# Rotary half swap by a copy and four transfers, and token factors spread by transpositions, in a two-block transformer kernel

## The chip, the cores and the metric

The kernel runs on one core of one Trainium2 chip. The metric is the device time of one execution in microseconds; lower is better. Several runs are taken, and their median is quoted.

## The reference, cut to what matters

512 tokens of width 1024 go through two transformer blocks in float32. Two pieces of it matter here: the rotary turn of queries and keys in the first block, and the root-mean-square norms, which stand in both.

```python
def rmsnorm(x, g):
    return x * rsqrt(mean(x * x, axis=-1) + EPS) * g

def apply_rope(t, cos, sin):            # t: 64 features of one half head
    t1, t2 = jnp.split(t, 2, axis=-1)   # 32 and 32
    return jnp.concatenate([t1 * cos - t2 * sin, t1 * sin + t2 * cos], axis=-1)

def first_block(x, ...):
    h = rmsnorm(x, norm_mix_g); proj = h @ w_in
    p, q, k, v = split(proj, [512, 1024, 1536])
    pool_out = multiscale_pool(p, pool_w, pool_scale)
    q, k = apply_rope(q), apply_rope(k)             # 4 heads, 2 x 64 features each
    attn_out = diff_attention(q, k, v, lam, ...)
    x = x + concat([pool_out, attn_out]) @ w_o
    u = causal_dwconv(rmsnorm(x, norm_ffn_g) @ w_up, conv_w, conv_b)
    x = x + (silu(gate) * val) @ w_down
    return rmsnorm(x, norm_final_g)
# second block: feed forward, sparse attention and recurrence side by side,
# feed forward, gated embedding; each with a norm before and a norm behind it
```

## The kernel before, in words

Features lie on the 128 partitions and the 512 tokens along the row, so a block of 128 output features is one PSUM bank of 128x512. The phases in the names of tiles are mixa (mixer of the first block), ffna (its feed forward), fin (its last norm), ffn (the two feed forwards of the second block), mixb (its mixer) and ple (the end). Each float32 weight is split into two float32r parts, hi by a cast on ScalarE (ACT) and lo by a subtraction on VectorE (DVE), in `chunk()` (line 550); each activation likewise in `split()` (line 565). A block of features is then three matmuls for each 128 rows of the weight (`three()`, line 577).

A norm's factor is a value for each token. It is made with tokens on partitions: a matmul with a column of ones sums the squares (`colsum()`, line 672), DVE scales it, GpSimd (POOL) raises it to the power -0.5 (`pow()`, line 679), and `bcast()` (line 696) spreads it back along the row, the same on every partition. For each column of 128 tokens `bcast()` issues one float32 matmul: the column, broadcast to 128x128, is the stationary operand, and the identity moves. It is called with four columns in first_mix, first_ffn, final_norm, second_mix and in each of the two ffn, and with two columns for each half of the tokens in each of the three `renorm()` (line 719): 6 x 4 + 3 x 2 x 2 = 36 products.

`rope()` (line 773) makes the rotary turn of one block of 128 features: two half heads of 64, each of two groups of 32. It needs the block with those groups swapped in pairs. The PSUM block p is split into hi (ACT) and lo (DVE), two matmuls with a permutation matrix `permr` as stationary operand add up the swapped block in another PSUM bank, and DVE makes three passes: p by cos, swapped by sin, and their sum. It runs eight times in first_mix, for query and key of four heads; `permr` is loaded by the SP queue and cast by ACT in `later()` (line 510).

`attention()` (line 800) takes the turned query and key of a head: score products, the maximum on DVE, exponents on ACT, transpositions on TensorE (PE), and the products with the values. Beside the heads, first_mix has the value product (`tokens()`, line 621), four pooling groups and the output product.

No order of work is written by hand. The calls of `Net` are recorded in a `Plan` (line 161). `simulate()` (line 250) is a list scheduler over a cost for each instruction (lines 207 to 233) and a lag between engines (lines 148 and 149): on every engine it takes next the instruction that can start first, and among those that can start at once the one with the smallest key. A DMA costs its issuing queue 470 ns, lands after its bytes at 380 B/ns and 1700 ns more. It runs twice, first with weights for nothing and then with weights placed by what the first pass found, and `write()` emits each engine's instructions in that order. At run time every engine works strictly through its own list. All of them are emitted from line 444, so the profile's rows are told apart by their tiles, and all tiles of 128x512 in SBUF are named slot.

Of the kernel before, what the change touches and what calls it, by code (L numbers as in the profile page):

```python
# [13 lines left out]
OP = mybir.AluOpType  # L14
# [23 lines left out]
class View:  # L38
    """a tile, or a part of one, that gets its place when the program is written out"""
# [22 lines left out]
    def parts(self):  # L62
        b = self.base
        if b.parts is None:
            return [b]
        return [p for p, some in zip(b.parts, (self.dummy.min() < b.at, self.dummy.max() >= b.at)) if some]
# [58 lines left out]
class Base:  # L125
# [5 lines left out]
    def halve(self, at):  # L131
        """from here on the columns before and behind this one are written and read apart"""
        self.at, self.parts = at, [Part(), Part()]
# [27 lines left out]
class Plan:  # L161
    """records instructions, orders them by a model of the core's engines, then writes them out"""
# [8 lines left out]
    def add(self, engine, call, args, kw):  # L171
# [38 lines left out]
        if o.call[1] == "dma_start":  # L210
            o.bytes = int(np.prod(out.dummy.shape if isinstance(out, View) else ins[0].dummy.shape)) * 4
            o.cost, o.lag = 470, 1700
        else:
            o.bytes = 0
            o.lag = 200
            psum = any(v.base.pool == "ps" for _, v in views)
            if engine == "tensor":
                r = all(v.base.dt == F32R for v in ins)
                wide = args[1].n
                o.cost = 3 + (128 * 2 if call == "transpose" else max(n, 2 * wide) if r else 4 * max(n, wide)) / 2.4  # L220
            elif engine == "scalar":
                o.cost = (51 if psum else 93) + n / 1.2 + 93 * sum(k in ("bias", "scale", "accum_out") for k, _ in views)
                f = [x for x in list(args) + list(kw.values()) if isinstance(x, AF)]
                o.func = SETS.get(f[0]) if f else None
            elif engine == "vector":
                fast = not psum and call in ("tensor_copy", "tensor_scalar", "memset")
                cols = sum(v.n == 1 < n for v in ins) if call in ("scalar_tensor_tensor", "tensor_scalar") else 0
                o.cost = 69 + 61 * cols + max([n] + [v.n for v in ins]) / (1.92 if fast else 0.96)
                if call == "tensor_tensor_reduce":
                    o.cost += 270  # L230
            else:
                per = {"memset": 1, "affine_select": 1, "tensor_tensor": 2.6, "tensor_copy": 4}.get(call, 2)
                o.cost = 230 + n * per / 1.2 + (n * 165 if kw.get("op") == OP.pow else 0)
# [3 lines left out]
    # ordering  # L237
# [12 lines left out]
    def simulate(self, first):  # L250
        """list scheduling: sets o.start; the order of starts"""
# [195 lines left out]
class Net:  # L447
# [8 lines left out]
    # tiles  # L456
# [6 lines left out]
    def halved(self, x, at=T // 2):  # L463
        x.base.halve(at)
        x.dummy = np.broadcast_to(np.arange(x.dummy.shape[1], dtype=np.int16), x.dummy.shape)
        return x
# [18 lines left out]
    # constants  # L485
    def setup(self):
# [16 lines left out]
        for _ in range(WARM):  # opens the clock gate of the array  # L503
            nc.tensor.matmul(p, self.ident, self.ident, start=True, stop=True)
# [5 lines left out]
    def later(self):  # L510
        """what the first products do not wait for"""
# [3 lines left out]
        perm = self.t("perm", 1, (P, P))  # L515
        nc.sync.dma_start(perm, a["perm"])
        self.perm = self.c([P, P], "permr", F32R)
        nc.scalar.copy(self.perm, perm)
# [7 lines left out]
    def held(self, w, K, behind):  # L526
        """like chunk(), in slots: the parts of K blocks"""
# [21 lines left out]
    # weights: two float32r parts whose sum is the float32 weight  # L549
# [15 lines left out]
    def split(self, x, g=None, to=None):  # L565
        """x (times the column g) in two float32r parts"""
# [16 lines left out]
    def dots(self, p, q, k, s, t, L):  # L583
        """queries t..L on partitions, keys before L"""
        (qh, ql), (kh, kl) = q, k
        for i, (x, y) in enumerate(((qh, kh), (qh, kl), (ql, kh))):
            self.nc.tensor.matmul(p, x[s, t:L], y[s, :L], start=i == 0, stop=i == 2)

    def block(self, xs, w, p=None):
        """one block of 128 output features in PSUM; w: [P, K * 128] in DRAM"""  # L590
# [12 lines left out]
    def both(self, xs, ws, ps, held=None):  # L603
        """blocks of 128 output features: step by step all of them for one half of the tokens"""
# [16 lines left out]
    def tokens(self, xs, w, n, whole=False, cut=False):  # L621
        """n output features, tokens on partitions: four PSUM banks; w: [chunks, P, k * n]; whole: so many blocks of
        tokens at a time; cut: the last block by halves of the features"""
# [34 lines left out]
    # norms; with a side: for one half of the tokens  # L658
    def sumsq(self, acc, x, scale=1.0, side=None):
        """acc: the sums of squares, made by the first call for each side"""  # L660
# [23 lines left out]
    def mean(self, p, scale=1.0 / 1024, under=None, out=None):  # L684
        """p * scale + EPS (times under)"""
# [10 lines left out]
    def bcast(self, r, keep=False):  # L696
        """column values on tokens -> [P, n * 128], the same on every partition"""
        nc = self.nc
        p = self.sm()[:, :r.n * P]
        for c in range(r.n):  # L700
            nc.tensor.matmul(p[:, c * P:(c + 1) * P], r[:, c:c + 1].to_broadcast([P, P]), self.ident,
                             start=True, stop=True)
# [6 lines left out]
    def prenorm(self, g):  # L709
        """split parts of h * g; the mean square with EPS, and its root's inverse for each token"""  # L710
# [8 lines left out]
    def renorm(self, ys, acc, g, under, gpre, late):  # L719
        """h += g * norm(ys), where ys lack the factor under ** -0.5; then prenorm(gpre); both by halves, each when  # L720
        late() has made its part of ys"""
# [17 lines left out]
    # first block  # L739
# [33 lines left out]
    def rope(self, p, cos, sin):  # L773
        nc = self.nc
        q, u = self.slot(), self.slot()
        hi, lo = self.split(p)
        pp = self.sm()
        nc.tensor.matmul(pp, self.perm, hi, start=True, stop=False)
        nc.tensor.matmul(pp, self.perm, lo, start=False, stop=True)
        nc.vector.tensor_tensor(u, p, cos, op=OP.mult)  # L780
        nc.vector.tensor_tensor(q, pp, sin, op=OP.mult)
# [3 lines left out]
    def diff_lambda(self):  # L785
# [12 lines left out]
        return lam  # minus lambda  # L798
# [35 lines left out]
    def headnorm(self, po):  # L834
        """the inverse root of the mean square of each token, for four blocks of tokens"""
# [7 lines left out]
    def turned(self, o):  # L843
        """tokens on partitions -> features on partitions"""
# [93 lines left out]
    def final_norm(self, gnext):  # L938
        """h <- norm(h) * g, with the next norm's split parts and factor"""
# [20 lines left out]
    # second block  # L960
# [92 lines left out]
    def select_keys(self, b, qi, kT, widx):  # L1053
        """0 on the selected keys of query block b, -NEG elsewhere"""
# [79 lines left out]
    def gated(self, p, rs):  # L1134
        """silu(p * rs)"""
# [6 lines left out]
    def recurrence(self, h, q, f, v, gate, masks):  # L1142
        """per chunk of 128 tokens: products of f over ever longer runs of tokens; a pair of tokens s < t meets
        at the level where they lie in the two halves of one run"""
# [177 lines left out]
    def ple(self, xs, r):  # L1322
        """tokens on partitions"""
# [81 lines left out]
def constants():  # L1405
# [9 lines left out]
    perm = (p[:, None] == (p[None, :] ^ 32)).astype(f)  # L1415
# [8 lines left out]
    return {"cf": cf, "perm": perm, "onehot": onehot, "masks": np.concatenate(ms, 1).astype(np.uint32)}  # L1424


def pack(i):
    i = {k: np.asarray(v) for k, v in i.items()}

    def blocks(w):  # L1430
        """[K*128, M*128] -> [M, 128, K*128]"""
# [3 lines left out]
    def halves(w):  # L1435
        """blocks of the upper and of the lower half of the rows"""
# [3 lines left out]
    def wide(w, nch):  # L1440
        """[1024, n] -> [chunks, 128, k*n]"""
# [75 lines left out]
```

## Time and profile before

| | |
|---|---|
| median of 3 runs | 1773.06 us (1772.69 to 1775.02) |
| span of the profiled execution | 1772.8 us, 22576 instructions |
| PE busy | 1759.4 us (99%), 8882 matmul records |
| DVE, ACT, POOL busy | 1033.4 us, 715.1 us, 49.3 us |
| mean granted TensorE clock | 0.998 |
| DMA | 162.47 MB, all of the kernel's own on the queue of SP |

For the profiled execution the profile gives the span, from its first to its last instruction, and no other time; the median of the runs is 0.26 us above that span. A matmul's record is longer than the time until the next matmul can start, since matmuls are pipelined: what an instruction costs PE is read from the distance between the starts of neighbours, not from its record. In names of matmuls the moving operand stands first behind the arrow and the stationary one second.

### The profile page before, as it was taken

To read this page: it belongs to the slowest core of one execution; us is meant where nothing else is said; L and a number is where in the kernel's file an instruction comes from. 1 tells how busy PE (TensorE), PEld (TensorE's weight loads), DVE (VectorE), ACT (ScalarE), POOL (GpSimd) and SP (SyncE) were. 2 spreads that over 40 slices of the span, in tenths; PEclk is the share of its full clock that TensorE was granted. 3 is DMA by queue.
4 is the path that set the end of the run, shared out by engine and by line. 5 is a ranking of instruction groups with operands and counts; after the bars stand their busy time and mean duration, and the time that the engine had idled before them with its cause. 6 is when DMAs were issued, how large, how long until landed. Compare 5 with 4: busy or idle time off the path is not lost.

```text
span 1772.8 us, 22576 instructions
## 1 busy us (share of the span) xinstructions
PE 1759.4 (99%) x8882; PEld 1476.8 (83%) x8882; DVE 1033.4 (58%) x1820; ACT 715.1 (40%) x1248; POOL 49.3 (3%) x68
## 2 busy tenths in 40 slices
PE   9999999999999999999999999999999999999998
PEld 7778888888888888888898888788899888888896
DVE  7886776367655432343488999553657432343475
ACT  5664444234443322322355334553345322322364
POOL 0021000000000000000010000000000000000000
PEclk9999999999999999999999999999999999999999
DMA  5212232332233223332342321013331323322331
GB/s 201 72 53 92 94 96 77 113 107 96 77 103 106 95 73 106 107 97 83 111 130 71 95 84 49 13 48 95 97 130 49 104 75 101 112 95 80 113 105 60
DMA packets 51690, 162.47 MB, mean 92 GB/s; under 512 B 5936, under 2 KB 7552, under 8 KB 51584
## 3 DMA queue, kind: packets, MB, share of 16 engines
q1 hardware_dynamic: 51584, 161.04, 28.9%
q8 instruction: 69, 1.13, 0.3%
q14 instruction: 37, 0.30, 0.1%
HBM read 158.89 MB, written 2.12 MB: 91 GB/s over the span
## 4 chain that ended last, share of the span: by engine, by line
PE 94%; DVE 4%; ACT 0%; issue 0%; DMA 0%; SPq 0%; POOL 0%; POOLq 0%; DVEq 0%; ACTq 0%
PE ffn.mm L444 41%; PE ffna.mm L444 20%; PE mixb.mm L444 15%; PE mixa.mm L444 7%; PE mixb.sm L444 5%; PE ple.mm L444 3%; DVE mixb.slot L444 2%; PE mixa.sm L444 2%; DVE mixb.m L444 0%; PE ffn.sm L444 0%; DMA mixa.wr_52:2_113<-in_w1qk 0%; SPq L444 0%; PE ple.sm L444 0%; PE fin.sm L444 0%; DVE mixa.dsum L444 0%
## 5 line engine op out<-in xcount | busy, mean ns | idle before, releaser
L444 DVE TENSOR_TENSOR ffn.slot<-ffn.slot,ffn.mm 128x512 f32<-128x512 f32 (+1 forms) x68 | 42.4, 625 | 177.2 <-PE ffn.mm L444 176.5
L444 DVE TENSOR_TENSOR ffn.slot<-ffn.mm,ffn.slot 128x512 f32<-128x512 f32 x44 | 30.3, 691 | 110.4 <-PE ffn.mm L444 109.6
L444 PE MATMUL mixb.sm<-mixb.slot,mixb.slot 128*128 128x64 f32 (+6 forms) x496 | 73.6, 308 | 1.0 <-ACT mixb.slot L444 0.5
L444 DVE TENSOR_TENSOR mixb.slot<-mixb.slot,mixb.slot 128x256 f32<-128x256 f32 (+3 forms) x143 | 67.3, 495 | 11.6 <-ACT mixb.slot L444 11.0
L444 PEld LDWEIGHTS mixb.sm<-mixb.slot,mixb.slot 128*128 128x128 f32 (+1 forms) x496 | 61.1, 190 | 12.2 <-issue 3.3
L444 DVE SCALAR_TENSOR_TENSOR ffna.slot<-ffna.slot,cols,ffna.slot 128x511 f32<-128x511 f32 x88 | 65.8, 748 | 3.1 <-ACT ffna.slot L444 1.3
L444 DVE TENSOR_TENSOR ffna.slot<-ffna.mm,ffna.slot 128x512 f32<-128x512 f32 x44 | 30.3, 689 | 46.4 <-PE ffna.mm L444 45.8
L444 ACT ACTIVATE ffn.slot<-ffn.slot 128x512 f32<-128x512 f32 (+1 forms) x68 | 39.2, 578 | 40.0 <-DVE ffn.slot L444 39.8
L444 DVE TENSOR_TENSOR ffn.slot<-ffn.slot,ffn.slot 128x512 fp32r<-128x512 f32 (+2 forms) x94 | 52.0, 562 | 5.0 <-ACT ffn.slot L444 4.6
L444 ACT COPY mixb.slot<-mixb.sm 128x128 f32<-128x128 f32 (+6 forms) x75 | 27.1, 376 | 43.3 <-PE mixb.sm L444 43.0
L444 DVE TENSOR_TENSOR ffna.slot<-ffna.slot,ffna.slot 128x512 f32<-128x512 f32 (+1 forms) x51 | 35.3, 691 | 14.7 <-ACT ffna.slot L444 13.8
L444 DVE TENSOR_TENSOR mixb.slot<-mixb.mm,mixb.slot 128x512 f32<-128x512 f32 (+1 forms) x28 | 19.3, 690 | 41.7 <-PE mixb.mm L444 40.5
L444 ACT ACTIVATE ffna.slot<-ffna.slot,cols 128x512 f32<-128x512 f32 x44 | 35.8, 815 | 2.6 <-DVE ffna.slot L444 1.9
L444 ACT CAST ffna.slot<-ffna.slot 128x512 fp32r<-128x512 f32 x22 | 13.7, 621 | 52.3 <-DVE ffna.slot L444 52.3
L444 DVE TENSOR_TENSOR h<-h,ffna.mm 128x512 f32<-128x512 f32 x16 | 11.0, 687 | 39.8 <-PE ffna.mm L444 39.8
L444 ACT ACTIVATE ffna.slot<-ffna.slot 128x512 f32<-128x512 f32 x22 | 13.9, 632 | 40.1 <-DVE ffna.slot L444 38.5
L444 DVE SCALAR_TENSOR_TENSOR mixb.slot<-mixb.sm,ffn.rr,mixb.slot 128x128 f32<-128x128 f32 (+3 forms) x32 | 17.0, 546 | 19.6 <-PE mixb.sm L444 18.5
L444 ACT CAST ffn.slot<-ffn.slot 128x512 fp32r<-128x512 f32 x44 | 27.3, 622 | 2.4 <-DVE ffn.slot L444 1.4
L444 PE MATMUL mixa.sm<-mixa.slot,mixa.slot 128*128 128x128 f32 (+5 forms) x184 | 27.9, 322 | 0.0
L444 POOL TENSOR_TENSOR ffn.rr<-ffn.rv,mhalf 128x2 f32<-128x2 f32 x8 | 6.2, 779 | 736.1 <-DVE ffn.rv L444 736.1
L444 DVE MATCH_REPLACE8 mixb.slot<-mixb.m,mixb.slot 128x256 f32<-128x256 f32 (+2 forms) x48 | 26.1, 549 | 0.0
L444 PEld LDWEIGHTS mixa.sm<-mixa.slot,mixa.slot 64*128 64x128 f32 (+1 forms) x184 | 21.3, 187 | 5.4 <-issue 2.6
(2192 smaller groups left out, 5366.3 us busy)
## 6 DMA issues: line engine op xcount, KB each, us to landing
h<-in_x SPq DMA_DIRECT2D x8, 256.0 KB, 5.9
mixb.slot<-dv SPq DMA_DIRECT2D x8, 256.0 KB, 4.3
out_y<-ple.slot SPq DMA_DIRECT2D x8, 256.0 KB, 2.0
mixa.wr_43:1_83<-in_w1qk SPq DMA_DIRECT2D x1, 512.0 KB, 4.0
mixa.wr_52:2_113<-in_w1qk SPq DMA_DIRECT2D x1, 512.0 KB, 6.7
mixa.wr_65:3_169<-in_w1v SPq DMA_DIRECT2D x1, 512.0 KB, 5.6
mixa.wr_65:4_208<-in_w1v SPq DMA_DIRECT2D x1, 512.0 KB, 5.5
mixa.wr_65:5_248<-in_w1v SPq DMA_DIRECT2D x1, 512.0 KB, 5.1
```

Of the source, the lines that this page charges most:

```text
L444: getattr(getattr(nc, engine), call)(*[real(v) for v in o.args], **{k: real(v) for k, v in o.kw.items()})
```

## The change

`rope()` copies the PSUM block to SBUF on ACT (one copy of 128x512) and issues, from the queue of ACT, four DMAs of 32 partitions each (64 KB), SBUF to SBUF, that put each group of 32 features where its partner was; DVE then multiplies the swapped tile in SBUF by sin. The permutation matrix, its load, its cast, the two matmuls, the lo part and the second PSUM bank go. `bcast()` transposes the broadcast column against the identity, instead of multiplying. The planner learns tiles cut into four parts by partitions, so that each transfer is recorded as the writer of one part, and charges a DMA 100 ns where the issuing engine is not SP; no other DMA of the kernel is issued from another engine. The rest of the diff takes out comments and docstrings.

```diff
@@ View.parts
-        return [p for p, some in zip(b.parts, (self.dummy.min() < b.at, self.dummy.max() >= b.at)) if some]
+        lo, hi = self.dummy.min(), self.dummy.max()
+        return [p for p, x, y in zip(b.parts, (0,) + b.cuts, b.cuts + (1 << 15,)) if lo < y and hi >= x]
@@ Base
-    def halve(self, at):
-        self.at, self.parts = at, [Part(), Part()]
+    def cut(self, *cuts):
+        self.cuts, self.parts = cuts, [Part() for _ in range(len(cuts) + 1)]
@@ Plan.add
-            o.cost, o.lag = 470, 1700
+            o.cost, o.lag = 470 if engine == "sync" else 100, 1700
@@ Net
     def halved(self, x, at=T // 2):
-        x.base.halve(at)
+        x.base.cut(at)
...
+    def quarters(self, x):
+        x.base.cut(32, 64, 96)
+        x.dummy = np.broadcast_to(np.arange(P, dtype=np.int16)[:, None], x.dummy.shape)
+        return x
@@ Net.later
-        perm = self.t("perm", 1, (P, P))
-        nc.sync.dma_start(perm, a["perm"])
-        self.perm = self.c([P, P], "permr", F32R)
-        nc.scalar.copy(self.perm, perm)
@@ Net.bcast
         for c in range(r.n):
-            nc.tensor.matmul(p[:, c * P:(c + 1) * P], r[:, c:c + 1].to_broadcast([P, P]), self.ident,
-                             start=True, stop=True)
+            nc.tensor.transpose(p[:, c * P:(c + 1) * P], r[:, c:c + 1].to_broadcast([P, P]), self.ident)
@@ Net.rope
-        q, u = self.slot(), self.slot()
-        hi, lo = self.split(p)
-        pp = self.sm()
-        nc.tensor.matmul(pp, self.perm, hi, start=True, stop=False)
-        nc.tensor.matmul(pp, self.perm, lo, start=False, stop=True)
+        q, u, t, w = self.slot(), self.slot(), self.slot(), self.quarters(self.slot())
+        nc.scalar.copy(t, p)
+        for i in range(4):
+            nc.scalar.dma_start(w[32 * i:32 * i + 32, :], t[32 * (i ^ 1):32 * (i ^ 1) + 32, :])
         nc.vector.tensor_tensor(u, p, cos, op=OP.mult)
-        nc.vector.tensor_tensor(q, pp, sin, op=OP.mult)
+        nc.vector.tensor_tensor(q, w, sin, op=OP.mult)
         nc.vector.tensor_tensor(q, q, u, op=OP.add)
```

## Rows read from the trace of the kernel before

**Rows 1.** Page, part 1: busy time and share of the span.

```profile
PE 1759.4 (99%) x8882; PEld 1476.8 (83%) x8882; DVE 1033.4 (58%) x1820; ACT 715.1 (40%) x1248; POOL 49.3 (3%) x68
```

**Rows 2.** Page, part 4: chain that ended last, by engine.

```profile
PE 94%; DVE 4%; ACT 0%; issue 0%; DMA 0%; SPq 0%; POOL 0%; POOLq 0%; DVEq 0%; ACTq 0%
```

**Rows 3.** Windows; us, then busy us (count) of PE, PEld, DVE, ACT, POOL, clock, DMA share, GB/s.

```profile
48.00:108.00 60.00, 59.56 (x346) 47.43 (x346) 51.66 (x137) 38.09 (x113) 2.03 (x2) 1.00 0.20 64
...
170.00:546.00 376.00, 376.00 (x1676) 311.90 (x1675) 240.80 (x313) 156.98 (x201) 1.77 (x2) 1.00 0.31 97
...
890.00:1190.00 300.00, 297.09 (x1855) 250.44 (x1854) 248.81 (x618) 146.71 (x348) 14.74 (x22) 0.99 0.22 68
```

**Rows 4.** Waits of PE: waiter, releaser, us, times, longest.

```profile
PE mixb.sm L444 <- DVE mixb.slot L444: 2.1, 4, 0.9
...
PE mixa.sm L444 <- DVE mixa.dsum L444: 0.4, 1, 0.4
```

**Rows 5.** Instructions by tile permr: count, ns min/median/max, first and last start.

```profile
L444 PE MATMUL mixa.sm<-mixa.slot,permr x16: 387/395/478, 21.6 to 103.0; 128*128 128x512 f32 x16
L444 ACT CAST permr<-mixa.perm x1: 284/284/284, 13.6 to 13.6; 128x128 fp32r<-128x128 f32 x1
```

**Rows 6.** Timeline of PE: start us, us, ..., count.

```profile
21.65 0.39 PE L444 MATMUL mixa.sm<-mixa.slot,permr 128*128 128x512 f32 x1
21.88 0.40 PE L444 MATMUL mixa.mm<-mixa.slot,mixa.wl_52:2_181 128*128 128x512 f32 x1
...
63.21 0.48 PE L444 MATMUL mixa.sm<-mixa.slot,permr 128*128 128x512 f32 x1
63.53 0.63 PE L444 MATMUL mixa.mm<-mixa.slot,mixa.wh_163:9_434 128*128 128x512 f32 x2
```

**Rows 7.** Tile ident: one row of transpositions, two of eight of factor products (72 records).

```profile
L444 PE MATMUL ple.sm<-ident,h x32: 270/272/273, 1705.3 to 1728.7; 128*128 128x128 f32 x32
...
L444 PE MATMUL ffn.sm<-ident,ffn.rr x16: 270/275/376, 893.5 to 1716.1; 128*128 128x128 f32 x16
...
L444 PE MATMUL mixa.sm<-ident,mixa.rr x8: 271/275/275, 27.8 to 28.6; 128*128 128x128 f32 x8
```

**Rows 8.** Timeline of PE around one spread of four columns.

```profile
27.80 1.05 PE L444 MATMUL mixa.sm<-ident,mixa.rr 128*128 128x128 f32 x8
28.60 0.48 PE L444 MATMUL mixa.mm<-mixa.wl_65:4_270,mixa.slot 128*128 128x512 f32 x1
```

**Rows 9.** Timeline of PE around sixteen transpositions.

```profile
1705.29 1.91 PE L444 MATMUL ple.sm<-ident,h 128*128 128x128 f32 x16
1706.95 0.48 PE L444 MATMUL ple.mm<-ple.wh_2103:313_13837,ffn.slot 128*128 128x512 f32 x1
```

**Rows 10.** Groups by form, 20 to 106 us, DVE and ACT: busy us, mean ns.

```profile
L444 DVE TENSOR_TENSOR mixa.slot<-mixa.sm,mixa.slot 128x512 f32<-128x512 f32 x8 | 5.5, 686 | 1.8 <-PE mixa.sm L444 1.8
L444 DVE TENSOR_TENSOR mixa.slot<-mixa.mm,mixa.slot 128x512 fp32r<-128x512 f32 x8 | 5.5, 684 | 0.0
...
L444 ACT CAST mixa.slot<-mixa.mm 128x512 fp32r<-128x512 f32 x7 | 4.1, 593 | 3.1 <-PE mixa.mm L444 2.8 <-DVE mixa.slot L444 0.3
```

**Rows 11.** Timeline of SP and tile answers: issue and landing of transfers.

```profile
910.10 3.69 SPq L444 DMA_DIRECT2D mixb.slot<-dv  x8
...
DMA to landing us min/median/max: 3.1/4.3/4.8
...
L444 SPq DMA_DIRECT2D out_y<-ple.slot x8: 332/333/344, 1752.2 to 1769.7; - x8
DMA to landing us min/median/max: 2.0/2.0/2.1
```

**Rows 12.** Timeline of ACT and DVE in one rotation (the key block of head 1).

```profile
62.24 0.58 ACT L444 CAST mixa.slot<-mixa.mm 128x512 fp32r<-128x512 f32 x1
...
63.59 1.28 DVE L444 TENSOR_TENSOR mixa.slot<-mixa.mm,mixa.slot 128x512 fp32r<-128x512 f32 x2
65.78 0.69 DVE L444 TENSOR_TENSOR mixa.slot<-mixa.sm,mixa.slot 128x512 f32<-128x512 f32 x1 [0.91 <-PE mixa.sm L444]
```

More of the change, by code (lines that the diff above doesn't have):

```diff
@@ L1414, in constants @@
         cf[:, 2 + 16 * g:18 + 16 * g] = (w / np.minimum(np.arange(16) + 1, w)).astype(f)
-    perm = (p[:, None] == (p[None, :] ^ 32)).astype(f)
     first = [0, 1, 2, 3, 4, 5, 6, 7, 8, 9, 10, 11, 12, 13, 14, 15, 16, 19, 21, 24, 27, 31, 35, 40, 46, 52, 59, 67,
@@ L1423, in constants @@
     ms = [(s // (2 * L) == j // L) & (s % (2 * L) < L) for L in LEVELS[:-2]] + [s == t]
-    return {"cf": cf, "perm": perm, "onehot": onehot, "masks": np.concatenate(ms, 1).astype(np.uint32)}
+    return {"cf": cf, "onehot": onehot, "masks": np.concatenate(ms, 1).astype(np.uint32)}
 def pack(i):
```

## The prediction

> **What bounds the kernel now.** I read the page's busy times first: PE is busy 1759.4 us of 1772.8 us, DVE and ACT far less [rows 1]. That a busy PE also sets the end is said by the chain of waits, which runs through PE for 94% of the span and through DVE for 4% [rows 2]. The table of stretches shows where that is less sure: in the mixer of the first block, 48 to 108 us, where six of the eight rotary turns lie, PE is busy 59.56 of 60 us, but DVE is at 51.66 and ACT at 38.09; from 170 us on a feed forward keeps PE at 376.00 of 376.00 us [rows 3]. Last, the waits of PE: the largest sum is 2.1 us, and in mixa the largest on DVE is 0.4 us [rows 4]. So the reader should see an engine that always has a product ready. What is taken from PE's list shortens the end by as much, as long as nothing new makes PE wait.
>
> **What goes from PE, the permutation.** There are 16 products with permr, from 21.6 to 103.0 us [rows 5]. Their records last 0.39 us, but the next matmul starts 0.23 us after them; behind a group of short ones it is 0.32 us [rows 6]. The 0.09 us more belongs to the change from short to long and passes on to the next long product. 16 x 0.23 = 3.7 us; with 0.32 us for all it would be 5.1 us, the upper end.
>
> **What goes from PE, the spreading.** The 36 float32 products show as 72 records, two for each [rows 7]. Four of them, eight records, hold PE from 27.80 to 28.60 us, 0.20 us for each product [rows 8]. The kernel already transposes float32 blocks against the same identity: one record each, and sixteen in a row hold PE from 1705.29 to 1706.95 us, 0.104 us for each [rows 9]. The saving is 36 x (0.20 - 0.104) = 3.5 us. These rows have a full block as stationary operand, not a broadcast column, so I keep bounds: nothing saved, if a transposition of a broadcast column also takes two passes, and 36 x 0.20 = 7.2 us, if it cost nothing. I take 3.5 us, because shape, type and identity are the same.
>
> The sixteen rows show a pitch of 0.104 us although each record is some 0.27 us long [rows 7, 9]. The Trainium skill (TensorE: Matmul & The Clock Gate, Part 4: PE-mode transpose) gives about 275 ns for a 128x128 transposition in a kernel's context. By that figure the 36 would take an estimated 9.9 us and the edit would lose 2.7 us; the trace agrees with the figure as a duration and not as a distance, and the distance is what PE pays.
>
> **What goes from DVE and ACT.** DVE loses eight subtractions of 684 ns, 5.5 us; the sin product stays at 686 ns, with its operand in SBUF instead of PSUM [rows 10]. Since PE waits 0.4 us for DVE in this stage, I count nothing for it. ACT makes a copy in place of the cast (593 ns, [rows 10]), the same size from the same bank. The load of the permutation on SP and its cast of 284 ns at 13.6 us [rows 5] also go, at nothing: PE is in the first blocks then and needs neither. Without the second PSUM bank and with the same count of SBUF tiles, no buffer gets scarcer. POOL's queue is passed by nothing.
>
> **What comes: 32 transfers on ACT's queue.** No row shows a DMA issued by ACT. SP's eight in a row took 3.69 us, 0.46 us each, and a single one 0.33 us [rows 11]. Four issues for each rotary turn are 1.3 us at 0.33 us; the ends are 0, if ACT issues beside its work, and 4 x 0.46 = 1.84 us. I take 1.3 us, as the single issue is nearest to one behind a copy. Behind them on ACT wait exponents, weight casts and casts of the next operands; DVE's subtractions and then PE's products wait for those. Six turns hold ACT 7.9 us in a stretch where it is idle for 60 - 38.09 = 21.9 us [rows 3]; this idle time hides the hold. If it were not there, 8 x 1.3 = 10.6 us would fall on the path.
>
> **When the swapped block is there.** Before, from the start of the cast at 62.24 us to the sin product at 65.78 us it took 3.54 us [rows 12]. After, it is a copy of 0.58 us, the issue of 1.3 us and a landing. The nearest rows for a landing are 2.0 us for 256 KB out of SBUF in the quiet end, and 4.8 us, the slowest of eight loads into SBUF in a crowd [rows 11]. I take 2.0 us, since the source is SBUF and the DMA share in 48 to 108 us is 0.20 [rows 3]: 3.9 us, 0.4 us later than before. The ends are 0.58 + 2.0 = 2.6 us (0.9 us earlier) and 0.58 + 1.84 + 4.8 = 7.2 us (3.7 us later). The key's turn comes last in a head, so this counts four times: 1.5 us, of which PE fills a part with other blocks. I charge 1.0 us of waiting.
>
> The rows show one transfer of 256 KB landing in the 2.0 us that I take for four of 64 KB. The Trainium skill (DMA: Bandwidth & Descriptors, Rules for kernel authors) says that transfers to disjoint partition halves serialize on the same engines and that one transfer of all partitions is better. That speaks against four parts; no run here yet shows it, and the second rival carries it in rows.
>
> **The sum.** 1772.8 - 3.7 - 3.5 + 1.0 = 1766.6 us of span; the median lies 0.26 us above the span shown, so I say 1766.9 us. A measurement can tell about 0.2%, 3.5 us, from no change: faster is below 1769.5 us, slower above 1776.6 us.
>
> **Rival 1, the transposition costs as much as its record.** If PE were held 0.27 us by each of the 36, the spreading would cost 36 x 0.07 = 2.5 us more instead of 3.5 us less: 1773.06 - 3.7 + 2.5 + 1.0 = 1772.9 us, no change. The pitch of the sixteen speaks against it [rows 9]. Chance 0.03.
>
> **Rival 2, the landing takes the permutation's gain back.** The four transfers pile up, the sin product at the head of DVE's list waits, and PE, which cannot pass over a score product, waits with it. Midway to the upper end, 1.85 us late in four heads, it is 7.4 us: 1773.06 - 7.2 + 7.4 = 1773.3 us, no change. For it: DVE is busy 51.66 of 60 us in that stretch [rows 3] and works in order. Against it: DVE loses 5.5 us, and the planner knows of 1.7 us and more until a landing and puts other products ahead. Chance 0.14.
>
> **Rival 3, ACT's queue becomes the bound, slower.** If each issue holds ACT 0.46 us and the list behind it has no slack there, because its order was planned with 100 ns for each, then 8 x 1.84 = 14.7 us land on PE: 1773.06 - 7.2 + 14.7 = 1780.6 us. It turns to slower from a loss of 7.2 + 3.5 = 10.7 us, 1.3 us for each turn. For it: the planned order falls short of the true issue time by up to 1.4 us a turn. Against it: ACT's 21.9 idle us. Chance 0.10.
>
> **How the numbers follow.** The forecast keeps 0.73. Its own range is 1762.5 to 1769.5 us: the 5.1 us for the permutation, some relief from DVE and an order of work that falls better on the low side, waits of 3.6 us on the high side. The order of work is planned anew, and in 890 to 1190 us PE has 2.9 us of idle time [rows 3], which may grow or shrink. The whole range is 1762.0 to 1772.5 us: about 0.04 lies below, the slower rival and the upper part of rivals 1 and 2, some 0.16, above. Faster 0.73, same 0.03 + 0.14 = 0.17, slower 0.10.
>
> **What would show each step.** Right: no record with permr; 36 records where there were 72, at a pitch near 0.10 us; PE's busy time less by about 7 us; PE waits in mixa still near 1 us; ffna beginning 4 us earlier and the rest 3.5 us more by the end. Rival 1 would show as a pitch of 0.27 us; rival 2 as waits of DVE on a DMA and of PE on DVE between 48 and 108 us; rival 3 as idle time of ACT behind its issues and waits of PE on ACT. The prediction is wrong if PE's busy time falls by 7 us and the span does not, or if the 0.10 us pitch doesn't hold for a broadcast column.

## The result, and the profile after

The changed kernel takes 1781.88 us (median; 1781.56 to 1784.4) against 1773.32 us before: ratio 1.0051, interval 1.0037 to 1.0065. It is 8.6 us slower, where 6 us faster was forecast. The page's busy times and its chain by engine:

```profile
PE 1759.2 (99%) x8830; PEld 1472.8 (83%) x8830; DVE 1030.9 (58%) x1812; ACT 714.7 (40%) x1247; POOL 48.6 (3%) x68
...
PE 91%; DVE 5%; ACT 1%; DMA 1%; issue 1%; ACTq 0%; SPq 0%; POOL 0%; DVEq 0%; POOLq 0%
```

52 records are gone from PE's list, as announced: 16 with permr and half of the 72 of the spreading. Yet PE's busy time is what it was [rows 1], and its share of the chain fell from 94% [rows 2] to 91%. Fewer products that keep PE busy as long are slower products. The table of stretches (columns as in [rows 3]) shows where:

```profile
48.00:108.00 60.00, 53.92 (x264) 40.88 (x263) 41.30 (x117) 33.60 (x97) 2.02 (x2) 0.86 0.23 72
...
52.80:59.60 6.80, 6.80 (x16) 4.64 (x16) 6.69 (x25) 4.27 (x15) 0.00 (x0) 0.50 0.14 53
...
76.70:80.10 3.40, 3.40 (x15) 2.33 (x13) 2.77 (x12) 2.44 (x9) 0.00 (x0) 0.50 0.38 137
100.60:107.40 6.80, 6.80 (x18) 4.45 (x17) 3.82 (x15) 3.63 (x14) 0.00 (x0) 0.50 0.00 0
```

In 48 to 108 us only 264 products fit where 346 did [rows 3]: PE is idle for 6.1 us instead of 0.4, and in three stretches, 17.0 us together, the granted clock is 0.50, the 1.2 GHz level; before, the whole stretch had 1.00. The waits of PE, and the stage's end, read off the first spreading in the next phase (columns as in [rows 5]):

```profile
PE mixa.sm L445 <- ACT mixa.slot L445: 5.2, 4, 2.6
...
PE mixa.sm L445 <- DVE mixa.slot L445: 1.8, 3, 0.9
```

```profile
L445 PE MATMUL ffna.sm<-ident,ffna.rr x4: 272/272/273, 198.7 to 199.0; 128*128 128x128 f32 x4
```

Before, the same tile's first record starts at 186.5 us. So the mixer of the first block ends 12.2 us later; 5.1 us of that come back by the end of the two executions (spans 1772.8 and 1779.9 us); the later spreadings are among them, and a stretch of 3.4 us at 0.50, from 1127.2 us on, that only the execution of before has. What the waits follow from stands in ACT's own timeline, for the turns of query and key in head 1 (start, duration, instruction, and in brackets the idle time before it and its releaser):

```profile
57.11 0.59 ACT L445 COPY mixa.slot<-mixa.mm 128x512 f32<-128x512 f32 x1
60.18 0.27 ACT L445 COPY mixa.slot<-mixa.sm 128x128 f32<-128x128 f32 x1 [2.49 <-PE mixa.sm L445]
60.24 0.53 ACTq L445 DMA_DIRECT2D mixa.slot<-mixa.slot  x1
...
61.80 1.80 ACTq L445 DMA_DIRECT2D mixa.slot<-mixa.slot  x3
63.65 0.48 ACT L445 COPY mixa.slot<-mixa.sm 128x384 f32<-128x384 f32 x1 [1.48 <-DMA mixa.slot<-mixa.slot]
...
64.97 0.59 ACT L445 COPY mixa.slot<-mixa.mm 128x512 f32<-128x512 f32 x1
65.59 0.51 ACTq L445 DMA_DIRECT2D mixa.slot<-mixa.slot  x1
66.15 0.59 ACT L445 COPY mixa.slot<-mixa.sm 128x512 f32<-128x512 f32 x1 [0.59 <-ACT mixa.slot L445]
68.65 0.62 ACT L445 CAST mixa.slot<-mixa.slot 128x512 fp32r<-128x512 f32 x1 [1.92 <-DVE mixa.slot L445]
68.66 1.81 ACTq L445 DMA_DIRECT2D mixa.slot<-mixa.slot  x3
```

The four issues of a turn don't stand together. The query's block is copied at 57.11 us; its first issue stands behind a copy that waits 2.49 us for PE, the other three follow at 61.80. Up to 59.6 us PE is at the 1.2 GHz level (the table above), so part of this wait belongs to the clock. The key's last three stand behind a cast of the query's turned block, which waits 1.92 us for DVE: the key's swap can't be issued before the query's turn is done. On DVE and PE this ends as follows (the first two rows are the sin product of the query and that of the key, the latter with the sum):

```profile
66.20 0.68 DVE L445 TENSOR_TENSOR mixa.slot<-mixa.slot,mixa.slot 128x512 f32<-128x512 f32 x1
...
72.34 1.42 DVE L445 TENSOR_TENSOR mixa.slot<-mixa.slot,mixa.slot 128x512 f32<-128x512 f32 x2 [0.49 <-DMA mixa.slot<-mixa.slot]
...
74.47 0.67 PE L445 MATMUL mixa.sm<-mixa.slot,mixa.slot 64*128 64x128 f32 x6 [2.64 <-ACT mixa.slot L445]
```

From copy to sin product it is 9.1 us and 7.4 us, where [rows 12] had 3.54. The transfers themselves (issue duration min/median/max in ns; then queue, size, median us to landing):

```profile
L445 ACTq DMA_DIRECT2D mixa.slot<-mixa.slot x32: 514/590/1555, 20.1 to 115.3; - x32
...
mixa.slot<-mixa.slot ACTq DMA_DIRECT2D x32, 64.0 KB, 2.1
```

### The profile page after: what moved, and what is told of

Its sections match the earlier page's. It is cut to its first block, busy times and chain, and to the rows that moved or that the text cites. A ratio compares the mean times of both kernels' runs of the same rounds, so it can differ in the third digit from the quotient of the medians.

```text
span 1779.9 us, 22508 instructions
## 1 busy us (share of the span) xinstructions
PE 1759.2 (99%) x8830; PEld 1472.8 (83%) x8830; DVE 1030.9 (58%) x1812; ACT 714.7 (40%) x1247; POOL 48.6 (3%) x68
## 4 chain that ended last, share of the span: by engine, by line
PE 91%; DVE 5%; ACT 1%; DMA 1%; issue 1%; ACTq 0%; SPq 0%; POOL 0%; DVEq 0%; POOLq 0%
PE ffn.mm L445 40%; PE ffna.mm L445 20%; PE mixb.mm L445 15%; PE mixa.mm L445 6%; PE mixb.sm L445 5%; PE ple.mm L445 3%; DVE mixb.slot L445 2%; PE mixa.sm L445 1%; DVE mixa.slot L445 1%; ACT mixa.slot L445 1%; DVE mixb.m L445 0%; DMA mixa.slot<-mixa.slot 0%; DMA mixa.wr_50:2_113<-in_w1qk 0%; PE ffn.sm L445 0%; PE ple.sm L445 0%
## 5 line engine op out<-in xcount | busy, mean ns | idle before, releaser
L445 DVE TENSOR_TENSOR mixb.slot<-mixb.mm,mixb.slot 128x512 f32<-128x512 f32 (+1 forms) x28 | 19.3, 688 | 42.1 <-PE mixb.mm L445 40.8
L445 PE MATMUL mixa.sm<-mixa.slot,mixa.slot 128*128 128x128 f32 (+5 forms) x184 | 31.9, 349 | 7.2 <-ACT mixa.slot L445 5.2
L445 PEld LDWEIGHTS mixa.sm<-mixa.slot,mixa.slot 64*128 64x128 f32 (+1 forms) x184 | 22.3, 199 | 14.7 <-ACT mixa.slot L445 9.9
L445 DVE TENSOR_TENSOR mixa.slot<-mixa.slot,mixa.slot 128x512 f32<-128x512 f32 (+1 forms) x37 | 26.2, 712 | 14.0 <-ACT mixa.slot L445 9.0
```

Of the source, the lines that this page charges most:

```text
L445: getattr(getattr(nc, engine), call)(*[real(v) for v in o.args], **{k: real(v) for k, v in o.kw.items()})
```

## The experiments

All times are medians; the kernel before had 1772.9 to 1773.1 us beside each. The edits are cut to the lines that matter.

### The parts alone, and the issues moved or planned

**e1**, only the transposition; **e2**, only the swap.

```diff
 # e1: before, with bcast() of the change
 # e2: the change, with bcast() of before
```

> The kernel before with the 36 spreading products as transpositions and the permutation products kept. Both theories: PE pays 36 x 0.10 us less, 3.5 us, and nothing new waits: 1769.8 us (1768.5 to 1771), gap between time and span as before, about 0.3 us. If the transposition were held for its record of 0.27 us, it would be slower by 2.5 us, 1775.8 us.

> The changed kernel with the spreading products put back as float32 matmuls: the swap by four transfers on the queue of ACT alone. If the two edits add up: the changed kernel plus 3.5 us, 1785.4 us (1783.5 to 1787.5), with PE waits of 6 to 8 us and a clock near 0.86 in the mixer of the first block. If the loss came from the two together (a new order of work), it would lie near 1770 us.

e1 1773.89 us (ratio 1.0002, 0.9993 to 1.0011), e2 1779.28 us (1.0033, 1.0021 to 1.0045). Neither is what its expectation said. The parts don't add up: the change costs 8.6 us, its parts 0.8 and 6.2 us. And e1, which only takes work from PE, gains nothing. In e1 PE is busy 58.16 us in 48 to 108 us, not 59.56 as in [rows 3], though no rotary turn was touched. What both share with the change is a new order of work: another price for an instruction makes the planner choose again everywhere.

**e3**, the planner told 600 ns for an issue on ACT; **e4**, the four transfers on SP's queue.

```diff
 # e3
-            o.cost, o.lag = 470 if engine == "sync" else 100, 1700
+            o.cost, o.lag = 470 if engine == "sync" else 600, 1700
 # e4
-            nc.scalar.dma_start(w[32 * i:32 * i + 32, :], t[32 * (i ^ 1):32 * (i ^ 1) + 32, :])
+            nc.sync.dma_start(w[32 * i:32 * i + 32, :], t[32 * (i ^ 1):32 * (i ^ 1) + 32, :])
```

> The changed kernel with the planner told 600 ns for a DMA issued by ACT instead of 100 ns; same instructions, another order. Theory A (the issues hold ACT's list for a time that the order did not plan for): the order spreads them and most of the 15 us comes back, 1768 to 1773 us, clock 1.0 in the mixer. Theory B (the way through SBUF takes too long whoever issues it and however it is planned): no more than 3 us come back, 1779 to 1783 us.

> The changed kernel with the four transfers issued from the queue of SP (planned at 470 ns each), so that ACT only makes the copy. Theory A (ACT's list is held): PE's waits in the mixer fall from 7 to under 2 us, the clock stays at 1.0, 1766 to 1770 us. Theory B (the landing, 2.1 us after the issue, is the cause): still over 1778 us. In either case, if the 1.7 us between span and time come from a second queue in use, they go back to 0.3 us.

e3 1772.83 us (0.9997, 0.9988 to 1.0006), e4 1773.12 us (1.0002, 0.9993 to 1.0011). Either takes 8.8 to 9.1 us back, e3 within the range of its theory A, e4 outside both of its ranges. That speaks for the issues on ACT, but both are planned anew, so neither tells the issues from the order. Neither median wins a microsecond over the kernel before, so something else holds the 7 us that were to be saved.

### Order and instruction told apart (e6, e7)

**e6** transposes but charges the old price, and **e7** multiplies but charges the new one. e6 has every engine's list as before, e7 every list of e1.

```diff
 # e6: before, with
+            o = nc.tensor.transpose(p[:, c * P:(c + 1) * P], r[:, c:c + 1].to_broadcast([P, P]), self.ident)
+            o.cost = 3 + 4 * P / 2.4
 # e7: before, with the product's
+            o.cost = 3 + 2 * P / 2.4
```

> The kernel before with bcast() transposing, but the planner still charges each transposition what it charged the fp32 product (216 ns), so that every engine's list is the one of before. Theory (the saving of 36 x 0.10 us is real, and e1 lost it because the planner's new price changed the order everywhere): 1773.1 - 3.5 = 1769.6 us, and the first 14 us keep PE at before's 11.8 us busy. Rival (a transposition of a broadcast column saves PE nothing that the neighbours do not take back at once): 1773.1, as in e1.

> The other corner: the fp32 products stay, but the planner is told 110 ns for each, so that the order is that of e1. No instruction differs from the kernel before. Theory (order costs 3.5 to 4 us by itself): 1773.9 + 3.5 = 1777.4 us, with the waits of e1 in the first 14 us and in mixa. Rival (the order costs nothing): 1773.1 to 1774.

| | old order | order by the new price |
|---|---|---|
| fp32 product | 1773.06 (before) | 1777.10 (e7) |
| transposition | 1769.74 (e6) | 1773.89 (e1) |

The four corners agree: the transposition saves 3.3 us in the one order and 3.2 us in the other, and the other order costs 4.0 to 4.2 us by itself. Ratios: e6 0.9979 (0.997 to 0.9988), e7 1.002 (1.0011 to 1.0029). In e6's timeline of PE four transpositions hold it from 28.39 to 28.75 us, 0.09 us each, where [rows 8] has 0.20:

```profile
28.39 0.60 PE L444 MATMUL mixa.sm<-ident,mixa.rr 128*128 128x128 f32 x4
28.75 0.48 PE L444 MATMUL mixa.mm<-mixa.wl_65:4_270,mixa.slot 128*128 128x512 f32 x1
```

**e8**, e3 with e6's price for the transposition, was to show whether that price disturbs e3 too.

```diff
 # e8: e3, with
+            o.cost = 3 + 4 * P / 2.4
```

> e3 (each issue on ACT planned with 600 ns) with the transposition charged as the product was. If the new price of the transposition is what disturbs the order in e3 too: e3's 1772.8 - 3.5 = 1769.3 us. If the swap's late landing in the order takes back what the permutation products gave: no better than e3, 1772 to 1774 us, with PE waiting for ACT and DVE in mixa again.

1773.14 us (0.9997, 0.9988 to 1.0006), as e3: that price is not what e3 loses by. What takes the saving back comes with the swap, by its transfers or by the order that it brings.

### More issues (e9)

```diff
-        for i in range(4):
-            nc.scalar.dma_start(w[32 * i:32 * i + 32, :], t[32 * (i ^ 1):32 * (i ^ 1) + 32, :])
+        for i in range(8):
+            nc.scalar.dma_start(w[16 * i:16 * i + 16, :], t[16 * (i ^ 2):16 * (i ^ 2) + 16, :])
```

> The changed kernel with eight transfers of 16 partitions for each rotation in place of four of 32, planned with 100 ns each as before: 32 more issues on ACT. Theory (the unplanned hold of ACT's list in mixa reaches PE): 32 x 0.5 = 16 us more hold; if half of it reaches PE, as in the changed kernel, 1781.9 + 8 = 1790 us, and up to 1798 us. Rival (the loss comes from the late landing or from the order alone, not from the hold): 1780 to 1784 us.

1793.95 us (1.0108, 1.0093 to 1.0124): 32 more issues cost 12.1 us, 0.38 us each, at 0.600 us of ACT each (median). Half the bytes in a transfer make an issue no shorter. The 12.1 us are not the issues alone: the order is planned anew here too, and the profiled execution is for 27.3 us at the 1.2 GHz level, that of the changed kernel for 17.0. PE's waits for ACT rise from 5.2 to 15.2 us in all:

```profile
PE mixa.sm L445 <- ACT mixa.slot L445: 15.2, 9, 3.2
```

### The loss taken apart in the changed kernel's own order (e10, e11, e16)

These keep every list of the changed kernel: an instruction is planned as before (`emit` is new) and another is written out in its place. e10 lets the sin product read a tile that is long there; e11 also leaves the issues out; e16 keeps the swap but issues from SP.

```diff
 # e10, e11
-        nc.vector.tensor_tensor(q, w, sin, op=OP.mult)
+        o = nc.vector.tensor_tensor(q, w, sin, op=OP.mult)
+        o.emit = [(*o.call, (q, cos, sin), o.kw)]
 # e11, for each dma_start
+            o.emit = []
 # e16, for each dma_start
+            o.emit = [("sync", "dma_start", o.args, o.kw)]
```

> The changed kernel with every engine's list as it is, the 32 transfers issued too, but the sin product reads the table of cosines in place of the swapped tile, so that nothing waits for a landing (the swap is left out of the result). Theory (most of the loss is the hold of ACT's list by the issues): 32 issues x 0.375 us, the slope of e9, is 12 us; without the landings only some 2 us come back: 1778 to 1781 us, and PE still waits for ACT in mixa. Rival (most of the loss is DVE waiting for a swapped block that lands late): back by 8 us or more, 1770 to 1774 us.

> The same, and the 32 transfers are left out of the program as well, the rest of every engine's list unchanged. What then remains against the kernel before is the saving of 7.2 us and the cost of the new order. Theory with an order that costs nothing: 1773.1 - 7.2 = 1766 us. With an order that costs what it did in e7, 4 us: 1770 us. If the landing and the hold were not the cause: above 1776 us.

> The changed kernel with every list as it is, but for the 32 issues, which are moved out of ACT's list to SP's queue at the same places of the written order. This takes the hold of ACT alone away and keeps the waits for the landings: e11 (neither hold nor landing, same order) has 1773.85, the changed kernel 1781.9. If the hold is most of the 8 us: 1774 to 1776 us. If the wait for the landing is most of it, whoever issues: 1778 to 1781 us.

e10 1775.95 us (1.0015, 1.0006 to 1.0024), e11 1773.85 us (1.0003, 0.9993 to 1.0012), e16 1776.36 us (1.0017, 1.0007 to 1.0026). Without the issues on ACT, but with the waits for the landings (e16), 5.5 us are back; without landings as well, another 2.5. The issues that still hold ACT in e10, where nobody waits for a landing, cost 2.1 us. So in this order the hold harms mostly together with the landing that it makes late: 2.1 us alone, 2.5 us for the waits alone, 8.0 us for both. Neither e10 nor e11 falls on a time that its expectation named. But e11 has no swap, no hold and 7 us less work on PE, and is not faster than before: this order costs more than those 7 us. Its rows, windows and waits, 48 to 108 us and all of mixa:

```profile
48.00:108.00 60.00, 55.56 (x299) 43.81 (x298) 47.28 (x129) 36.94 (x104) 2.40 (x2) 0.94 0.19 62
...
PE mixa.sm L446 <- ACT mixa.slot L446: 4.2, 4, 1.5
...
PE mixa.sm L446 <- DVE mixa.slot L446: 1.1, 2, 0.7
```

The first of these waits can be read off e11's timelines:

```profile
48.59 1.04 ACT L446 CAST mixa.wh_211:11_502<-mixa.wr_211:11_407 128x1024 fp32r<-128x1024 f32 x1 [1.21 <-PE mixa.mm L446]
49.54 0.61 ACT L446 CAST mixa.slot<-mixa.slot 128x512 fp32r<-128x512 f32 x1
...
47.81 0.69 DVE L446 TENSOR_TENSOR mixa.slot<-mixa.slot,mixa.slot 128x512 f32<-128x512 f32 x1
...
50.21 0.90 PE L446 MATMUL mixa.sm<-mixa.slot,mixa.slot 64*128 64x128 f32 x7 [1.43 <-ACT mixa.slot L446]
```

PE's next scores wait 1.43 us for a cast that has its operand from DVE by 48.50 us at the latest, but stands in ACT's list behind the cast of a weight, which itself waits 1.21 us for PE. The granted clock is 0.50 from 52.3 us on, for 6.8 us. e16 and the changed kernel show the same wait of 1.43 us (scores at 50.39 and 50.36 us) and a slow stretch of 6.8 us behind it. So this wait and this fall of the clock come with the order, not with the transfers.

### The swap in the order of before (e12 to e15, e17)

Here everything stands in the order of the kernel before, with e6's transposition. e12 writes out a copy with four transfers from SP where the cast stood, and leaves the lo subtraction and the products out; e13 issues from ACT instead; e14 has no transfer, and its sin product reads the PSUM block; e15 is e12 with the products kept as idle work; e17 makes the swap by two copies on ACT and two on DVE.

```diff
 # e12 (e13: "scalar")
+        nc.ops[n].emit = [(*nc.ops[n].call, nc.ops[n].args, nc.ops[n].kw)] + [
+            ("sync", "dma_start", (w[32 * i:32 * i + 32, :], hi[32 * (i ^ 1):32 * (i ^ 1) + 32, :]), {}) for i in range(4)]
+        for x in nc.ops[n + 1:n + 4]:                   # lo, two products (e15: lo alone)
+            x.emit = []
+        o.emit = [(*o.call, (q, w, sin), o.kw)]         # e14: p in place of w, and no transfers
 # e17
+        g = lambda i: (w[32 * i:32 * i + 32, :], p[32 * (i ^ 1):32 * (i ^ 1) + 32, :])
+        nc.ops[n].emit = [("scalar", "copy", g(i), {}) for i in (0, 1)]
+        nc.ops[n + 1].emit = [("vector", "tensor_copy", g(i), {}) for i in (2, 3)]
```

> e6 (transposition, order of the kernel before) in which also the swap is put in place into that order: the cast is a copy with four transfers on SP's queue right behind it, and the lo subtraction and the two permutation products are left out of the lists, everything else as before. Theory (the swap is worth 3.7 us on PE when neither ACT's list nor the order is disturbed, less a landing that is 1 us late in four heads): 1769.7 - 3.7 + 1 = 1767 us, at best 1766. Rival (the landing comes too late for the place that the order gives the sin product, and PE waits each time): 1770 to 1776 us.

> The same with the four transfers on ACT's queue, all four right behind the copy, so that they are not spread over ACT's list as in the changed kernel. The hold is four issues of 0.5 us, 2.0 us for each turn, in an order that left no room for it. Theory (the hold reaches PE by the slope of e9): e12 + 32 x 0.375 = e12 + 12 us, some 1779 us. Rival (it was the spreading of the issues over ACT's list, with waits between them, that cost; kept together they hide in ACT's idle time): within 2 us of e12.

> e12 (order of the kernel before, swap put in place) without its transfers, so that the sin product reads the unswapped block straight from PSUM (the swap is left out of the result): nothing waits for a landing and no queue holds an issue. Theory P (PE's list sets the end in the first mixer, so the 16 permutation products are worth their 3.7 us): 1769.7 - 3.7 = 1766 us. Theory C (that stage has a second chain, through exponents and copies on ACT, of nearly the same length, and the products only filled PE's waits for it): 1768.5 to 1771 us, with PE waiting for ACT in mixa as in e12.

> e12 with the two permutation products of each turn kept in PE's list as idle work whose result nobody reads (the sin product reads the transferred block, which here has the precision of the cast alone). Theory P: e12's 1772.7 + 3.7 = 1776.4 us. Theory C (the products fill waits, and keep the granted clock up): not slower than e12, 1769 to 1773 us, with less waiting of PE for ACT in mixa and a clock of 1.00 there.

> The order of the kernel before with transposition, no permutation products and a real swap, but without transfers: ACT copies two groups of 32 partitions from PSUM to their partners' places in SBUF where the cast stood, DVE the other two where the lo subtraction stood. If it is the landing (2.0 us and the issues) that costs e12 its 6.7 us over e14, and not the swap being made at all: a copy more on ACT (some 0.58 us) and one more on DVE (0.69 us) a turn, ready within 1.5 us, so 1766 to 1767.5 us, faster than both kernels. If any delay on ACT's and DVE's lists costs as much: 1770 to 1773 us.

| | us | ratio and interval | in mixa |
|---|---|---|---|
| e6, swap by products | 1769.74 | 0.9979 (0.997 to 0.9988) | PE idle 0.5 us in 48 to 108 us |
| e14, no swap | 1765.95 | 0.996 (0.9948 to 0.9973) | PE idle 0.5 us |
| e12, transfers from SP | 1772.68 | 0.9996 (0.9987 to 1.0005) | PE idle 3.3 us, clock 0.94 |
| e15, same and products kept | 1772.86 | 1.0001 (0.9992 to 1.001) | PE idle 2.2 us, clock 1.00 |
| e13, transfers from ACT | 1780.93 | 1.0049 (1.0036 to 1.0062) | PE idle 9.8 us, clock 0.97 |
| e17, copies | 1773.52 | 1.0002 (0.9993 to 1.0011) | PE idle 5.6 us, DVE 55.40 busy |

e14 is what theory P said: the products are worth 3.8 us on PE when nothing comes in their place. e15 is theory C: once the swap comes by transfers, the same products can be put back for 0.2 us. Both hold, each in its place, because the stage has two limits that lie close together. Part of what the products do in e15 is to keep the clock up: of e12's executions the three with a mean clock of 0.999 took 1770.9 to 1771.0 us, the others (0.996 to 0.998) up to 1774.9; e15 had 0.998 or more in all, and 1772.3 to 1773.8 us at 0.999. At the same clock, then, the products still cost near 2 us. How close the two limits lie shows in one turn of e12 against [rows 12]; the copy starts at the same 62.24 us:

```profile
62.24 0.58 ACT L447 COPY mixa.slot<-mixa.mm 128x512 f32<-128x512 f32 x1
...
62.85 2.41 SPq L447 DMA_DIRECT2D mixa.swap<-mixa.slot  x4
...
64.34 0.68 DVE L447 TENSOR_TENSOR mixa.slot<-mixa.mm,mixa.slot 128x512 f32<-128x512 f32 x1
66.82 0.69 DVE L447 TENSOR_TENSOR mixa.slot<-mixa.swap,mixa.slot 128x512 f32<-128x512 f32 x1 [1.79 <-DMA mixa.swap<-mixa.slot]
```

Four issues take 2.41 us, and the sin product starts at 66.82 instead of 65.78 us: 1.04 us late, with DVE standing still for 1.79. PE then waits for ACT, which waits for DVE:

```profile
PE mixa.sm L447 <- ACT mixa.slot L447: 3.0, 4, 1.2
```

In 48 to 108 us PE is idle for 2.8 us more than in e14, and the clock of 0.94 costs up to 0.06 x 60 = 3.6: together 6.4 of the 7.2 us between the two profiled executions (the medians are 6.7 us apart). e15, whose products keep PE working through part of the waits, has no slow stretch and the same time. In e13 the copy behind the issues waits 2.51 us, and e13 is 8.3 us slower than e12:

```profile
63.43 0.58 ACT L447 COPY mixa.slot<-mixa.mm 128x512 f32<-128x512 f32 x1
64.04 2.44 ACTq L447 DMA_DIRECT2D mixa.swap<-mixa.slot  x4
66.52 0.58 ACT L447 COPY mixa.slot<-mixa.sm 128x512 f32<-128x512 f32 x1 [2.51 <-issue]
...
PE mixa.sm L447 <- ACT mixa.slot L447: 11.0, 6, 2.1
```

So the rival to e13 falls too: kept together, the issues don't hide in ACT's idle time. The 8.3 us are not the hold alone, since e13's transfers also land after a median of 3.5 us, e12's after 2.0. e17 was to be the better version and isn't, a miss. Beside e14, which leaves the lo subtraction out, a turn has one copy more on ACT (578 ns) and two more on DVE (693 ns each), 15.7 us for eight, and 7.6 us of them reach the end. It needs no transfer at all to lose what the products gave. Its windows, beside e14's:

```profile
48.00:108.00 60.00, 54.41 (x302) 40.79 (x302) 55.40 (x141) 41.36 (x111) 2.03 (x2) 1.00 0.22 71
```

```profile
48.00:108.00 60.00, 59.50 (x346) 46.61 (x346) 50.87 (x147) 39.73 (x124) 3.03 (x3) 1.00 0.19 62
```

DVE has 4.5 us more to do, and PE is idle 5.1 us more, at a clock of 1.00. So it is not the landing as such: time added to the lists of DVE and ACT costs without one.

### The sum of the change

| step | us | from |
|---|---|---|
| kernel before | 1773.06 | |
| transposition | -3.3 | e6 |
| products and lo subtraction out | -3.8 | e14 - e6 |
| the changed kernel's order | +7.9 | e11 - e14 |
| waits for landings, issued from SP | +2.5 | e16 - e11 |
| issues on ACT's list | +5.5 | after - e16 |
| kernel after | 1781.88 | |

But for the row on the order, each step leaves the order of all else as it was. (In that row the sin product's operand also moves from PSUM to SBUF.) That order's 7.9 us are settled in part. Between the profiled executions of e14 and e11, 7.7 us apart, PE idles 3.9 us more in 48 to 108 us and has a stretch of 6.8 us at 0.50, which is 3.4 us of its work at most: together 7.3. One of the waits is explained above; the others are not. e6 is the only version measured that does the whole computation and beats both kernels.

The steps from the order's row on contain the clock too. Executions of one kernel differ in their mean granted clock, and in their time with it:

| | us at the highest clock | us at the lowest clock |
|---|---|---|
| e11 | 1771.5 and 1771.8 at 0.999 | 1775.1 and 1775.7 at 0.996 |
| e16 | 1774.5 at 0.999 | 1777.6 at 0.995 |
| e10 | 1773.1 at 0.999 | 1777.3 to 1777.7 at 0.996 |
| after | 1781.6 to 1784.4 at 0.994 (all four) | |

Each 0.001 goes with 0.8 us (e16) to 1.5 us (e10). The kernel before had 0.997 to 0.999, mostly 0.999, so an estimated 4 to 7 of the change's 8.6 us come with the 0.994. This can't be shared out exactly among the steps, since no execution of the changed kernel had a higher clock. Waits alone cost as well: e2's execution at 1.000, without a slow stretch, took 1777.3 us.

## Why the prediction was wrong

**The spreading** was right: 3.5 us forecast, 3.3 measured, at 0.09 us for each transposition against the 0.104 of [rows 9]. A broadcast column costs no second pass. Rival 1 is out.

**The permutation products** were right as a term of PE: 3.7 us forecast, 3.8 measured in e14.

**The hold of ACT** is the step that failed: the forecast put it at nothing, and it costs 5.5 us, the clock's part in it included (the changed kernel against e16). It was mis-sized: 0.33 us taken, 0.46 the upper end, 0.59 measured. The queue is no cause of the size: the same transfers take 0.582 us to issue on SP (e16). More important, "this idle time hides the hold" does not follow from 60 - 38.09 us. What ended ACT's idle time before (48 to 108 us, columns as in [rows 4]):

```profile
ACT mixa.slot L444 <- PE mixa.sm L444: 13.6, 11, 2.7
ACT mixa.slot L444 <- DVE mixa.dsum L444: 3.1, 5, 1.7
```

The idle time of ACT in this stage is time in which its next instruction waits for PE or DVE, in a ring: turn, scores, maximum, exponents, next operands. It is no reserve that a later instruction could use, since each engine's list is worked in order. Of the time added to these lists 43 to 63% reach the end in three runs (8.3 of 19.3 us in e13, 7.6 of 15.7 in e17, 12.1 of 19.2 in e9), in e13 and e9 with later landings or more slow stretches among them; the 11% of e10 (2.1 of 19.2), where nobody waits for a landing, is the exception.

**The landing** was right for a single transfer, a median of 2.1 us where 2.0 was taken; but waiting for it was charged with 1.0 us and costs 2.5 (e16 against e11). The lateness, forecast as 0.4 us in four heads, is 1.04 us in e12 for the turn shown, since four issues take 2.41 us and not 1.3. In the changed kernel it is 3.8 and 5.6 us for the two turns shown, because the four issues are scattered among instructions that wait. That an order planned with 100 ns would do this was seen for rival 3, but only as missing room, not as separation.

**The order** was named only as a spread in the range. It was put at nothing, and it is a term as large as the others: 4.0 us in e7, where no instruction differs, and 7.9 us here. A planner that orders by prices turns a price into a change of the whole list.

**The clock** was in no term. A stage that kept PE at 59.56 of 60 us had no slow stretch; with waits of up to 2.6 us in it the granted clock was at the 1.2 GHz level for 17.0 us. That is 8.5 us of PE's work at most. It explains why its busy time didn't fall: 7.2 us of work went, and 13.6 us more at half the clock (17.0 against the 3.4 in before) put 6.8 back. The line that said what would prove the forecast wrong expected PE's busy time to fall by 7 us.

**The rivals.** Rival 3 had the sign and nearly the number, 1780.6 for 1781.9 us, and its mechanism: PE waits for ACT, ACT idles behind issues. Its reckoning, 14.7 us of hold falling straight on PE, was not how it went: 5.5 us come from the issues, and the order's 7.9 us stand in no term of it, so that the near number is luck. Rival 2 is there too, with 2.5 us in this order. The chance of 0.10 rested on the 21.9 us of idle time alone.

**The base.** The statement that the median lies 0.26 us above the span compared two executions. In all runs the time is 1.7 to 1.8 us above the span of the same execution (1781.64 and 1779.9 us for the one shown), so the profiled execution of before took an estimated 1774.5 us. With the sum taken from the median this moved nothing.

## What to carry to other kernels

Before an operation is moved to an engine because that engine shows idle time, look at what ends that idle time: where it is another engine in the same loop, the time is latency of the loop and not room, and of a microsecond added there about half came out at the end here. An issue on a compute engine's queue is an instruction of that engine's list, so price it as measured (e3) or put it on a queue on which no compute waits (e4, e16); keeping the issues of a step together on ACT did not help (e13). Where a planner orders the work, test an instruction and its price apart, as in the table of e6 and e7: the order alone can be worth more than the edit.

## What the runs showed of the hardware

- An issue of a 64 KB transfer of 32 partitions within SBUF takes a median of 0.59 us on ACT and 0.58 on SP, and 0.60 us with half the bytes; single stores of 256 KB to memory took SP 0.33 [rows 11]. The same issue on ACT has a median of 0.515 us in e3, whose order spreads the issues. The four issues of a turn (2.41 us) last longer than one landing (2.0 us). The Trainium skill (DMA: Bandwidth & Descriptors, Issuing engines are not separate DMA queues) says that the time to initiate a transfer is usually small relative to the transfer. Here the trace differs: 0.58 against 2.0 us, and four in a row are the larger part of the way.
- The Trainium skill (DMA: Bandwidth & Descriptors, Rules for kernel authors) advises one transfer of all 128 partitions in place of two to disjoint halves, because the halves share the same engines. Here more parts did cost more, but not by the landing, whose median stayed at 2.0 us: eight for four cost 12.1 us, with their issues and the order planned for them. No run tried one transfer for all.
- Where PE waited in mixa, up to 2.6 us at a time, the granted clock went from 1.00 to 0.50 (the 1.2 GHz level) for 3.4 or 6.8 us at a time, in e9 once for 10.2. The sum of the waits doesn't foretell it: from 48 to 108 us e17 had 5.6 us of idle time and kept 1.00, e12 had 3.3 us and a mean of 0.94.
